# A two-layer decoder in fp32 on one core: up tiles of seven products stay in PSUM, and GpSimd makes one low half of the weights per up tile

## The chip, the cores and the metric

The kernel runs on one core of a Trainium2 chip. A core has five engines with a queue each: TensorE (PE, matrix products, which are written to PSUM alone), VectorE (DVE), ScalarE (ACT), GpSimd (POOL) and SyncE (SP, which here only starts DMAs). A queue runs its instructions in the order in which they stand. The metric is the device time of one execution in microseconds (us), as a median of several runs.

## The reference, cut to what matters

512 tokens of 1024 features pass two layers. Each has a token mixer, a gated MLP with a causal convolution, and a gated embedding. The change touches the MLP alone:

```python
def conv_ffn(xn, w_up, conv_w, conv_b, w_down):
    h = xn @ w_up                                    # 1024 -> 2 * 2816
    hp = jnp.pad(h, ((0, 0), (CONV_WIDTH - 1, 0), (0, 0)))
    c = conv_b + sum(hp[:, t:t + S] * conv_w[t] for t in range(CONV_WIDTH))   # width 3
    g, u = jnp.split(c, 2, axis=-1)
    return (jax.nn.silu(g) * u) @ w_down             # 2816 -> 1024
```

Everything is fp32.

## The kernel before

**Products in three matmuls.** Features lie on partitions and tokens along the free axis. Every operand x is kept as a high half (x rounded to a format that TensorE takes at full rate) and a low half (x minus that), and one product is three matmuls: high by high, high by low, low by high (`mm3`, line 234).

**Weights.** A table, `pieces`, lists every weight block in the order of its use. `load` brings a piece of up to 1 MB into one of three staging buffers (`wraw`, L173, queue SP). `pump` turns it into *units* of up to 128x1024, four units ahead of TensorE: ScalarE writes the high half (`wh`, L203), VectorE subtracts it for the low half (`wl`, L204). There are four buffers of each (WBUFS = 4), so a unit can be split only when TensorE has finished the one four before.

**Up tiles.** The MLP has 22 up tiles j per layer, each with 256 rows of `w_up`: 128 for the gate (s = 0) and 128 for the line (s = 1). Half of them (`UPS`: 7, 8, 9, 10, 12, 14, 16, 17, 18, 20, 21) are made by seven products of halves instead of eight, in `woven_up`; VectorE then also makes sums of weight blocks (`wsum`, L163 to L165). Products 1, 6, 7 and 4 are added up, in this order, in the left half of one PSUM bank (`ux`, in the code `chain`); 2 and 3, and 5, go to the halves of another (`uy`). After product 7 and after product 4 the running sum is read out by ScalarE with its sign turned (`minus`, L555), into an SBUF tile `line`; after products 1 and 6 it is copied into `head` (traced as `gate`). VectorE adds the rest (L816, L817). TensorE's order in such a tile is 1, 2, 6, 5, 7, 3, 4, twelve matmuls of 256 columns each. The other tiles have eight products' worth, 48 matmuls of 512 columns into the banks `up`, s = 0 first.

**Convolution.** `gated` takes the two halves, in PSUM for the ordinary tiles and in SBUF for those by seven products: ScalarE writes c = w2 * x + b (L761), VectorE adds two shifted taps to it (L763), for s = 0 and then for s = 1. Silu (L769), and VectorE's product with the line (L770), give the activation `a`.

**Down projection.** The tiles go in three parts: 0 to 7, 8 to 15 and 16 to 21. For the first two, activations are paired: `Pair.begin` and `Pair.end` make differences of the halves of two tiles (`act_3t`, `act_3u` for the fourth pair) and split each into high and low halves (ScalarE L311, VectorE L312). `woven_add` then takes seven products again, into `dx` and `dy`. Before it runs, the first up tile of the next part (8, and 16) is made with `later=True`: its products come before the down projection, its convolution inside it. The third part goes through `dense_add` (`d`), whose last factor is the activation of tile 21.

**What sets the order.** The code is recorded once, and a scheduler puts each engine's instructions in an order by its own estimate of times; `behind` adds an order between two instructions without a wait. At the seam of parts 1 and 2 it mixes the matmuls of tile 8 with the first ones of `dx` and `dy`. PSUM has eight banks, taken in turn.

Names in the profile leave out the numbers of buffers: `wl` is any unit's low half.

Of the kernel before, what the change touches and what calls it, by code (L numbers as in the profile page):

```python
# [13 lines left out]
P = 128  # L14
D = 1024
S = 512
# [7 lines left out]
ASIDE = {7: 12, 9: 7, 17: 7, 20: 6}  # L24
# [28 lines left out]
def tile_yoco(ctx: ExitStack, tc: tile.TileContext, t, out: bass.AP, out_b: bass.AP):  # L53
# [86 lines left out]
    raws, ready, splits, sums = {}, {}, {}, {}  # L140
    state = {"raw": 0, "unit": 0, "next": 0, "tags": [0, 1, 2], "turn": 2, "pt": 0, "sent": {}}
# [13 lines left out]
    def weave(i, q):  # L155
# [10 lines left out]
        return (g[:, 0:3:2], sums[i][:, 2:4], sums[i][:, 0:2], g[:, 3:4])[q]  # L166

# [11 lines left out]
    def pump(upto):  # L179
        while state["unit"] < min(upto, len(units)):  # L180
# [23 lines left out]
            state["split"] = splits[u] = cast, nc.vector.tensor_sub(low, src, hi.bitcast(F32))  # L204
# [77 lines left out]
    for i in range(IDLE):  # L282
        nc.tensor.matmul(ps, idle, idle.rearrange("p (o t) -> p o t", o=1).to_broadcast([P, 4, P]),
                         start=True, stop=True)
    minus_half = const.tile([P, S // 64], F32, name="minus_half")
# [445 lines left out]
    def ffn(l, norm, nxt):  # L731
# [23 lines left out]
        def gated(j, pss, fronts=()):  # L755
            cs = []
            for s, ps in enumerate(pss):
                col = s * NJ + j
                cw = [v("conv_w", (l * 3 + i) * 2 * NJ + col) for i in range(3)]
                c = tp.tile([P, S], F32, tag=f"c{s}", name=f"c{j}_{s}")  # L760
                nc.scalar.activation(c, ps, AF.Identity, bias=v("conv_b", l * 2 * NJ + col), scale=cw[2])  # L761
                for tap in (1, 2):
                    ins = nc.vector.scalar_tensor_tensor(c[:, tap:], ps[:, : S - tap], cw[2 - tap], c[:, tap:],  # L763
                                                         op0=ALU.mult, op1=ALU.add)
# [23 lines left out]
        def woven_up(j, later):  # L788
# [853 lines left out]
```

## Time and profile before

| | |
|---|---|
| median of 3 runs | 1098.21 us (1097.75 to 1098.51) |
| the profiled execution's own time | 1098.29 us |
| its span | 1096.6 us, granted TensorE clock 0.998 |
| busy: PE / DVE / ACT / POOL | 1087.3 / 958.1 / 660.1 / 124.9 us |
| low halves `wl` on DVE (two groups of the page) | 217.4 + 102.7 us in 198 + 84 instructions |
| first MLP, up tiles to the end of the down projection | about 156 to 498 us |
| second MLP | about 700 to 1045 us |

A row of the profile's tables reads: line, engine, operation, output <- inputs, shapes, count, busy time, mean duration of one in ns, idle time of the engine before them and what ended it. In a timeline, a row has its start, its duration, and in brackets the idle time before it. A matmul's row is longer than the distance to the next one, since matmuls overlap.

### The profile page before, as it was taken

To read this page: it belongs to the slowest core of one execution; us is meant where nothing else is said; L and a number is where in the kernel's file an instruction comes from. 1 tells how busy PE (TensorE), PEld (TensorE's weight loads), DVE (VectorE), ACT (ScalarE), POOL (GpSimd) and SP (SyncE) were. 2 spreads that over 40 slices of the span, in tenths; PEclk is the share of its full clock that TensorE was granted. 3 is DMA by queue.
4 is the path that set the end of the run, shared out by engine and by line. 5 is a ranking of instruction groups with operands and counts; after the bars stand their busy time and mean duration, and the time that the engine had idled before them with its cause. 6 is when DMAs were issued, how large, how long until landed. Compare 5 with 4: busy or idle time off the path is not lost.

```text
span 1096.6 us, 17486 instructions
## 1 busy us (share of the span) xinstructions
PE 1087.3 (99%) x6629; PEld 974.9 (89%) x6629; DVE 958.1 (87%) x1540; ACT 660.1 (60%) x1141; POOL 124.9 (11%) x192
## 2 busy tenths in 40 slices
PE   9999999999999999999999999999999999999997
PEld 7888988899999999988888887888999989999886
DVE  5598889989899989977988997799998999899787
ACT  5744665566576656655656775565665666567544
POOL 2200200000100010021114452000001000100200
PEclk9999999999999999999999999999999999999999
DMA  8621684124633267353234216441255333674634
GB/s 311 123 83 39 172 271 138 55 77 117 154 115 110 85 162 217 122 193 113 66 88 135 78 58 220 183 154 39 77 143 127 116 116 85 156 221 143 203 94 99
DMA packets 47508, 144.24 MB, mean 132 GB/s; under 512 B 13048, under 2 KB 18688, under 8 KB 36928
## 3 DMA queue, kind: packets, MB, share of 16 engines
q1 hardware_dynamic: 40560, 128.77, 35.7%
q0 software_dynamic: 5296, 9.70, 6.6%
q10 hardware_dynamic: 1568, 4.65, 1.1%
q8 instruction: 52, 0.85, 0.3%
q14 instruction: 32, 0.26, 0.1%
HBM read 116.89 MB, written 18.88 MB: 124 GB/s over the span
## 4 chain that ended last, share of the span: by engine, by line
PE 92%; DVE 2%; SPq 2%; issue 2%; DMA 1%; ACT 1%; POOL 0%; POOLq 0%; DVEq 0%; ACTq 0%
PE up L234 20%; PE ux L234 12%; PE dx L234 10%; PE uy L234 9%; PE dy L234 7%; PE d L234 4%; PE q L234 4%; PE gate L234 4%; PE u L234 4%; PE o L234 4%; PE up L751 2%; SPq L1399 2%; PE pv L1331 1%; PE v L244 1%; PE v L245 1%
## 5 line engine op out<-in xcount | busy, mean ns | idle before, releaser
L204 DVE TENSOR_TENSOR wl<-wraw,wh 128x1024 fp32r<-128x1024 f32 (+2 forms) x198 | 217.4, 1103 | 43.9 <-ACT wh L203 40.9
L203 ACT CAST wh<-wraw 128x1024 fp32r<-128x1024 f32 (+2 forms) x197 | 182.7, 932 | 105.8 <-PE up L234 21.5
L203 ACT CAST wh<-wsum 128x1024 fp32r<-128x1024 f32 x84 | 88.3, 1051 | 55.3 <-issue 14.9
L204 DVE TENSOR_TENSOR wl<-wsum,wh 128x1024 fp32r<-128x1024 f32 x84 | 102.7, 1226 | 17.7 <-ACT wh L203 14.3
L763 DVE SCALAR_TENSOR_TENSOR c<-up,vec,c 128x511 f32<-128x511 f32 (+1 forms) x88 | 65.1, 745 | 1.9 <-ACT c L761 1.5
L234 PE MATMUL up<-nf00h,wh 128*128 128x512 f32 x160 | 62.3, 390 | 0.0
L234 PE MATMUL up<-nf10h,wh 128*128 128x512 f32 x160 | 62.3, 390 | 0.0
L234 PE MATMUL up<-nf10l,wh 128*128 128x512 f32 x160 | 62.3, 389 | 0.0
L234 PE MATMUL up<-nf00l,wh 128*128 128x512 f32 x160 | 62.3, 389 | 0.0
L234 PE MATMUL up<-nf00h,wl 128*128 128x512 f32 x160 | 62.1, 389 | 0.0
L234 PE MATMUL up<-nf10h,wl 128*128 128x512 f32 x160 | 62.0, 389 | 0.0
L599 POOL DMA_DIRECT2D saved<-head x16 | 13.9, 870 | 412.5 <-DVE head L721 303.1
L163 DVE TENSOR_TENSOR wsum<-wraw 128x1024 f32<-128x1024 f32 x42 | 51.3, 1221 | 1.5 <-DMA wraw<-in_w_up 0.9
L761 ACT ACTIVATE c<-up,vec 128x512 f32<-128x512 f32 x44 | 33.9, 776 | 29.5 <-PE up L234 24.3
L234 PE MATMUL ux<-t,wh 128*128 128x256 f32 x264 | 50.8, 285 | 0.0
L234 PEld LDWEIGHTS ux<-t,wh 128*128 128x128 f32 x264 | 41.1, 192 | 0.8 <-ACT line L555 0.6
L234 PE MATMUL ux<-t,wl 128*128 128x256 f32 x132 | 37.4, 283 | 0.0
L234 PEld LDWEIGHTS up<-nf10h,wl 128*128 128x128 f32 x160 | 30.0, 188 | 6.3
L234 PEld LDWEIGHTS up<-nf00h,wl 128*128 128x128 f32 x160 | 30.0, 188 | 6.3
L234 PEld LDWEIGHTS up<-nf00l,wh 128*128 128x128 f32 x160 | 30.1, 188 | 6.1
L234 PEld LDWEIGHTS up<-nf10h,wh 128*128 128x128 f32 x160 | 30.0, 188 | 6.1
L234 PEld LDWEIGHTS up<-nf00h,wh 128*128 128x128 f32 x160 | 30.0, 188 | 6.1
(769 smaller groups left out, 3736.8 us busy)
## 6 DMA issues: line engine op xcount, KB each, us to landing
wraw<-in_w_up SPq DMA_DIRECT2D x44, 1024.0 KB, 5.1
wraw<-in_w_down SPq DMA_DIRECT2D x16, 1024.0 KB, 4.9
wraw<-in_w_gate SPq DMA_DIRECT2D x8, 1024.0 KB, 5.5
wraw<-in_w_down SPq DMA_DIRECT2D x8, 768.0 KB, 4.4
wraw<-in_w_u SPq DMA_DIRECT2D x4, 1024.0 KB, 9.2
wraw<-in_w_out SPq DMA_DIRECT2D x4, 1024.0 KB, 5.2
saved<-head POOLq DMA_DIRECT2D x16, 256.0 KB, 4.1
saved<-tail POOLq DMA_DIRECT2D x16, 256.0 KB, 4.1
```

The source lines that it names most:

```text
L163: nc.vector.tensor_add(s[:, 0::3], g[:, 1:2].to_broadcast([P, 2, k, P]), g[:, 0::3])
L203: cast = nc.scalar.copy(hi, src)
L204: state["split"] = splits[u] = cast, nc.vector.tensor_sub(low, src, hi.bitcast(F32))
L234: return [nc.tensor.matmul(ps, w, x, start=first and j == 0, stop=last and j == len(todo) - 1, skip_group_check=onto) for j, (w, x) in enu ...
L244: nc.tensor.matmul(ps, xh[:, s], wh[:, a:b], start=st, stop=False)
L245: nc.tensor.matmul(ps, xl[:, s], wh[:, a:b], start=False, stop=False)
L599: box["onto"] = nc.gpsimd.dma_start(x, y, accum_op=ALU.add)
L751: nc.tensor.matmul(ps, w[:, off + s * P : off + (s + 1) * P], x, start=k == 0 and x is xh and w is wh, stop=k == KD - 1 and x is xl)
L761: nc.scalar.activation(c, ps, AF.Identity, bias=v("conv_b", l * 2 * NJ + col), scale=cw[2])
L763: ins = nc.vector.scalar_tensor_tensor(c[:, tap:], ps[:, : S - tap], cw[2 - tap], c[:, tap:], op0=ALU.mult, op1=ALU.add)
L1331: nc.tensor.matmul(ps, lhs, rhs, start=j == 0, stop=j == len(todo) - 1)
L1399: nc.sync.dma_start(y[SQ * b : SQ * (b + 1), :, a, :], x[SQ * a : SQ * (a + 1), b::NQ].rearrange("p b m d -> p b (m d)"))
```

## The change

1. **Tiles by seven products stay in PSUM.** ScalarE's read-outs after product 7 is now a plain copy within the bank `ux`, from its left half to its right one. The one after product 4 is gone: the sum stays where it is. VectorE adds `side` and `head` in place, in PSUM (the first of them only after product 4 has ended). The line therefore keeps its sign, and `minus_w`, a negated copy of the convolution weights, made once by GpSimd, is used for it. The SBUF tiles for four of these outputs (`ASIDE`) are gone.
2. **One low half per up tile moves to GpSimd.** Except for tiles 6, 8, 15 and 16, the next unit's low half is a GpSimd subtraction that starts together with the taps (36 in all: 18 in each layer, of which 17 are 128x1024 and one 128x768). VectorE copies one column to `sign` when ScalarE has written the line's c, and GpSimd waits for that copy.
3. **The taps of these tiles stand together**, with high priority, in the order s = 0, s = 1, s = 0, s = 1, all behind `sign`, thus behind both of ScalarE's results.
4. Two small GpSimd instructions elsewhere (`prs`, `rows`) are put behind the last moved subtraction.

```diff
+OPEN = (6, 15)
@@ pump
-            state["split"] = splits[u] = cast, nc.vector.tensor_sub(low, src, hi.bitcast(F32))
+            held = low, src, hi.bitcast(F32)
+            if state["keep"] == u:
+                state["held"], state["keep"], splits[u] = held, None, (cast, None)
+            else:
+                start = shadows.pop(u, None)
+                lows = lowered(held, start) if start else nc.vector.tensor_sub(*held)
+                state["split"] = splits[u] = cast, lows
@@ new
+    def after(ins, front):
+        tc.add_manual_dep(ins.ins, front.ins.name,
+                          mybir.DependencyInfo(mybir.DependencyClass.Sync, mybir.DependencyReason.DATA),
+                          reason="start")
+    def lowered(held, start):
+        ins = box["lowered"] = nc.gpsimd.tensor_sub(*held)
+        after(ins, start)
+        return ins
@@ gated
+                if s and j in UPS:
+                    cw = [minus_w[:, (l * 3 + i) * NJ + j : (l * 3 + i) * NJ + j + 1] for i in range(3)]
                 nc.scalar.activation(c, ps, AF.Identity, bias=v("conv_b", l * 2 * NJ + col), scale=cw[2])
-                for tap in (1, 2):
-                    ins = nc.vector.scalar_tensor_tensor(c[:, tap:], ps[:, : S - tap], cw[2 - tap], c[:, tap:],
-                                                         op0=ALU.mult, op1=ALU.add)
-                    if fronts and tap == 1:
-                        behind(ins, splits[fronts[s]][1])
+                taps += [(c, ps, tap, cw[2 - tap]) for tap in (1, 2)]
...
+            if fronts or j in OPEN:
...
+            else:
+                with tc.high_priority():
+                    ins = nc.vector.tensor_copy(sign, cs[1][:, :1])
+                    if j in UPS:
+                        lowered(state["held"], ins)
+                    else:
+                        shadows[state["unit"]] = ins
+                    for x in taps[::2] + taps[1::2]:
+                        ins, front = tap(*x), ins
+                        behind(ins, front)
@@ woven_up
-            chain, other = psum(f"ux{j}")[:, first], psum(f"uy{j}")
-            if j in ASIDE:
-                head, tail = couple(ASIDE[j], f"out{j}", F32)
-            else:
-                head, tail = (tp.tile([P, S], F32, tag="hs", name=f"{x}{j}") for x in ("gate", "line"))
+            line, other = psum(f"ux{j}"), psum(f"uy{j}")
+            chain = line[:, first]
+            head = tp.tile([P, S], F32, tag="hs", name=f"head{j}")
...
             product(7, chain, w, 0, first=False)
-            minus(tail[:, second], chain)
+            nc.scalar.copy(line[:, second], chain)
             product(3, other[:, second], w, n, first=False)
-            product(4, chain, unit(), 0, first=False)
-            minus(tail[:, first], chain)
-            nc.vector.tensor_sub(tail[:, second], tail[:, second], side)
-            nc.vector.tensor_add(head, head, other)
-            return (head, tail) if later else gated(j, (head, tail))
+            if not later and j not in OPEN:
+                state["keep"] = state["unit"]
+            ends = product(4, chain, unit(), 0, first=False)
+            nc.vector.tensor_add(other, other, head)
+            after(nc.vector.tensor_add(line[:, second], line[:, second], side), ends[-1])
+            return (other, line) if later else gated(j, (other, line))
```

**What moves on VectorE.** This is VectorE's queue at the seam of parts 1 and 2 in the first layer, while TensorE makes tile 8: the rest of tile 7 (`c7`, `a7`), the pair's differences and low halves (`act0_3t`, `act0_3u`, `act0_3_0` to `_2`), the weight sums for `dx` (`wsum28`) and the low half of the first down unit (`wl59`). Before:

```order
L763 SCALAR_TENSOR_TENSOR c7_1_2429<-out7_2306,vec_84,c7_1_2429 128x511
L163 TENSOR_TENSOR wsum28_2487<-wraw28_2483 128x2x512
L763 SCALAR_TENSOR_TENSOR c7_1_2429<-out7_2306,vec_84,c7_1_2429 128x510
L164 TENSOR_TENSOR wsum28_2487<-wsum28_2487,wraw28_2483 128x512
L770 TENSOR_TENSOR a7_2433<-a7_2433,c7_1_2429 128x512
L165 TENSOR_TENSOR wsum28_2487<-wsum28_2487,wraw28_2483 128x512
L532 TENSOR_TENSOR act0_3t_2301<-a7_2433,a6_2297 128x256
L533 SCALAR_TENSOR_TENSOR act0_3u_2439<-act0_3t_2301,a7_2433 128x256
L204 TENSOR_TENSOR wl59_2486<-wraw28_2483,wh59_2485 128x1024
L535 SCALAR_TENSOR_TENSOR act0_3u_2439<-act0_3u_2439,a7_2433 128x256
L312 TENSOR_TENSOR act0_3_0_2436<-a7_2433,act0_3_0_2436 128x512
L312 TENSOR_TENSOR act0_3_1_2437<-act0_3t_2301,act0_3_1_2437 128x512
```

There the third `wsum` and `wl59` stand ahead of all three low halves of the pair; another row for the third low half, and then the next `wl`, follow. Now:

```order
L220 TENSOR_TENSOR wl58_2463<-wraw27_2350,wh58_2462 128x512
L805 TENSOR_TENSOR a7_2442<-a7_2442,c7_1_2434 128x512
L169 TENSOR_TENSOR wsum28_2495<-wraw28_2491 128x2x512
L550 TENSOR_TENSOR act0_3t_2310<-a7_2442,a6_2306 128x256
L551 SCALAR_TENSOR_TENSOR act0_3u_2448<-act0_3t_2310,a7_2442 128x256
L170 TENSOR_TENSOR wsum28_2495<-wsum28_2495,wraw28_2491 128x512
L553 SCALAR_TENSOR_TENSOR act0_3u_2448<-act0_3u_2448,a7_2442 128x256
L330 TENSOR_TENSOR act0_3_0_2445<-a7_2442,act0_3_0_2445 128x512
L330 TENSOR_TENSOR act0_3_1_2446<-act0_3t_2310,act0_3_1_2446 128x512
L171 TENSOR_TENSOR wsum28_2495<-wsum28_2495,wraw28_2491 128x512
L330 TENSOR_TENSOR act0_3_2_2447<-act0_3u_2448,act0_3_2_2447 128x512
L220 TENSOR_TENSOR wl59_2494<-wraw28_2491,wh59_2493 128x1024
```

Ahead of these stand the four taps of tile 7 in a row, and `wl57`, which stood before the first tap, is gone to GpSimd. `wl58` has come behind the taps, and `wl59` behind all three low halves of the pair and the third `wsum`.

**What moves on TensorE.** The matmuls of the same place, from the end of tile 8's product 3 (`uy8`), before:

```order
L234 MATMUL uy8_2450<-nf00l7_1001,wh57_2406 128x256
L234 MATMUL uy8_2450<-nf00h7_1000,wl57_2407 128x256
L234 MATMUL dx0_2567<-edge0_1756,wl59_2486 128x256
L234 MATMUL dx0_2567<-edge0_1756,wh59_2485 128x256 x2
L234 MATMUL dx0_2567<-edge0_1756,wl59_2486 128x256
L234 MATMUL dx0_2567<-edge0_1756,wh59_2485 128x256 x2
L234 MATMUL dx0_2567<-edge0_1756,wl59_2486 128x256
L234 MATMUL dx0_2567<-edge0_1756,wh59_2485 128x256 x2
L234 MATMUL dx0_2567<-edge0_1756,wl59_2486 128x256
L234 MATMUL dy0_2568<-act0_0_0h_1844,wl59_2486 128x256
L234 MATMUL ux8_2449<-t06_1957,wh58_2454 128x256
L234 MATMUL ux8_2449<-t07_1958,wh58_2454 128x256
```

Ten matmuls of `dx0` (of which the first reads `wl59`) and one of `dy0` stand between product 3 and product 4 (`ux8<-t...`). Now:

```order
L251 MATMUL ux8_2458<-t06_1963,wh58_2462 128x256
L251 MATMUL ux8_2458<-t07_1964,wh58_2462 128x256
L251 MATMUL ux8_2458<-t06_1963,wl58_2463 128x256
L251 MATMUL ux8_2458<-t02_2141,wh58_2462 128x256
L251 MATMUL ux8_2458<-t03_2142,wh58_2462 128x256
L251 MATMUL ux8_2458<-t02_2141,wl58_2463 128x256
L251 MATMUL ux8_2458<-t0_m5_1772,wh58_2462 128x256 x2
L251 MATMUL ux8_2458<-t0_m5_1772,wl58_2463 128x256
L251 MATMUL ux8_2458<-t0_rh_1949,wh58_2462 128x256
L251 MATMUL ux8_2458<-t0_rl_1950,wh58_2462 128x256
L251 MATMUL ux8_2458<-t0_rh_1949,wl58_2463 128x256
L251 MATMUL dx0_2574<-edge0_1760,wl59_2494 128x256
```

Product 4's twelve matmuls come first, one `dy0` matmul behind product 3, and the ten of `dx0`, beginning with `wl59`, behind them. Tile 8 of the second layer has the same two orders.

More of the change, by code (lines that the diff above doesn't have):

```diff
@@ L23 @@
 UPS = (7, 8, 9, 10, 12, 14, 16, 17, 18, 20, 21)
-ASIDE = {7: 12, 9: 7, 17: 7, 20: 6}
+OPEN = (6, 15)
 PAIRS = 4
@@ L139, in tile_yoco @@
     units = [(i, q, lo, n) for i, p in enumerate(pieces) for q, (lo, n) in enumerate(p[2])]
-    raws, ready, splits, sums = {}, {}, {}, {}
-    state = {"raw": 0, "unit": 0, "next": 0, "tags": [0, 1, 2], "turn": 2, "pt": 0, "sent": {}}
+    raws, ready, splits, sums, shadows = {}, {}, {}, {}, {}
+    state = {"raw": 0, "unit": 0, "next": 0, "tags": [0, 1, 2], "turn": 2, "pt": 0, "sent": {}, "keep": None, "held": None}
     def behind(ins, front):
@@ L284, in tile_yoco @@
                          start=True, stop=True)
+    sign = const.tile([P, 1], F32, name="sign")
     minus_half = const.tile([P, S // 64], F32, name="minus_half")
@@ L755, in gated @@
         def gated(j, pss, fronts=()):
-            cs = []
+            cs, taps = [], []
             for s, ps in enumerate(pss):
@@ L1427, in tile_yoco @@
     whole_f = whole.bitcast(F32)
-    nc.gpsimd.memset(rows.bitcast(F32), 0.0)
+    behind(nc.gpsimd.memset(rows.bitcast(F32), 0.0), box["lowered"])
     def bias_rows():
```

13 lines of the change are left out of this document (12 added, 1 removed).

## The prediction

> **What bounds the kernel now.** I read the page's busy totals first, then the waits of TensorE over the whole trace, then the two MLPs as windows.
>
> ```profile
> PE 1087.3 (99%) x6629; PEld 974.9 (89%) x6629; DVE 958.1 (87%) x1540; ACT 660.1 (60%) x1141; POOL 124.9 (11%) x192
> ...
> PE 92%; DVE 2%; SPq 2%; issue 2%; DMA 1%; ACT 1%; POOL 0%; POOLq 0%; DVEq 0%; ACTq 0%
> ```
>
> ```profile
> PE idle L283 <- DVE minus_half L286: 1.1, 1, 1.1
> PE dx L234 <- ACT head L701: 0.5, 1, 0.5
> PE sc L1263 <- PE sc L1264: 0.2, 1, 0.2
> ```
>
> ```profile
> 160.00:498.00 338.00, 338.00 (x2243) 312.17 (x2242) 307.68 (x426) 206.27 (x323) 21.00 (x23) 1.00 0.43 131
> 704.00:1045.00 341.00, 341.00 (x2256) 314.65 (x2256) 313.81 (x439) 209.27 (x329) 21.33 (x22) 1.00 0.44 132
> ```
>
> TensorE carries 92% of the chain of waits and itself waits 1.1 + 0.5 + 0.2 = 1.8 us in the whole run. In the windows (busy PE, PEld, DVE, ACT, POOL, then the clock) it is busy for all of 338.00 and 341.00 us at full clock. VectorE is at 307.68 of 338 us, 91%, but nobody waits for it there. Taking work from VectorE can therefore gain nothing; what the change can do is make TensorE wait. So I look for places where TensorE now gets its operand just in time and the new order delivers it later.
>
> **The change part by part.** *No more and no less for TensorE*: the same matmuls, hence 0.
>
> *VectorE's relief*: 34 low halves of 1024 and 2 of 768 columns, at the starting distance of such a subtraction (1.22 us for 1024; some 0.9 for 768), are 34 x 1.22 + 2 x 0.9 = about 43 us off VectorE. They lie beside matmuls: 0. ScalarE's 22 dropped read-outs: 0 for the same reason.
>
> *GpSimd's subtractions.* The trace has none of 1024 columns. The nearest rows:
>
> ```profile
> L1155 POOL TENSOR_TENSOR diff<-vd,diff 128x64 fp32r<-128x64 f32 x12 | 4.1, 355 | 0.2
> ```
>
> ```profile
> 522.50 1.33 POOL L342 TENSOR_TENSOR n1acc<-n1acc,n1sq 128x512 f32<-128x512 f32 x1 [3.85 <-ACT n1sq L337]
> 537.02 1.29 POOL L342 TENSOR_TENSOR n1acc<-n1acc,n1sq 128x512 f32<-128x512 f32 x1 [3.83 <-ACT n1sq L337]
> ```
>
> From 64 to 512 columns it is (1.29 - 0.355) / 448 = 2.1 ns a column, so 1024 columns take 1.29 + 512 x 0.0021 = 2.4 us. What runs beside them matters:
>
> ```profile
> 522.60 2.32 DVE L204 TENSOR_TENSOR wl<-wraw,wh 128x1024 fp32r<-128x1024 f32 x1
> ...
> 537.06 0.68 DVE L925 TENSOR_TENSOR z<-gate,np0rstd 128x512 f32<-128x512 f32 x1
> ```
>
> Both run beside a GpSimd addition. The subtraction with both sources in SBUF took 2.32 us, 1.1 more than its kind; the product that reads PSUM took its usual 0.68. The taps now read PSUM, and four of them take 4 x 0.66 = 2.64 us, longer than the 2.4. So I cost the pairing at 0. If GpSimd overhangs by up to 0.5 us, VectorE's next instruction is late by as much; at most tiles nobody notices: even where two tiles with seven products follow each other, the moved unit is wanted four products later (4 x 1.44 = 5.8 us after the end of product 4), and GpSimd ends at about 1.4 + 2.4 = 3.8. As bounds: 0, and 0.5 us at a place that is already late.
>
> *Taps from PSUM instead of SBUF.* These rows give both sources:
>
> ```profile
> L763 DVE SCALAR_TENSOR_TENSOR c<-up,vec,c 128x511 f32<-128x511 f32 x44 | 32.7, 746 | 1.6 <-ACT c L761 1.5
> L763 DVE SCALAR_TENSOR_TENSOR c<-gate,vec,c 128x511 f32<-128x511 f32 x14 | 10.5, 749 | 0.0
> ```
>
> 746 ns from PSUM (`up`) and 749 from SBUF (`gate`): no difference, 0. The Trainium skill, "VectorE: DVE Perf Modes", section "The TRN2 errata — SBUF-src ops pay a fixed extra latency per instruction", gives a vector instruction 58 cycles of access from SBUF and 120 from PSUM, by my estimate 65 ns more per tap at its 0.96 GHz, or 0.26 us per layer at the place below, and about 1101.6 us. The two rows show none of it.
>
> *Place A: the seam of parts 1 and 2, in each layer.* Here tile 7's convolution, the pair's differences and the first down unit meet. Before, in TensorE's chain, in TensorE's timeline, and on VectorE and ScalarE (first layer):
>
> ```profile
> 238.74 2.87 PE ux L234 x24
> ...
> 249.26 1.25 PE dx L234 x10
> ```
>
> ```profile
> 248.98 0.28 PE L234 MATMUL uy<-nf00h,wl 128*128 128x256 f32 x1
> 249.10 0.36 PE L234 MATMUL dx<-edge,wl 128*128 128x256 f32 x1
> ...
> 250.46 0.44 PE L234 MATMUL ux<-t,wh 128*128 128x256 f32 x2
> ```
>
> ```profile
> 240.93 0.75 DVE L763 SCALAR_TENSOR_TENSOR c<-out,vec,c 128x511 f32<-128x511 f32 x1
> 241.59 0.69 DVE L204 TENSOR_TENSOR wl<-wraw,wh 128x512 fp32r<-128x512 f32 x1
> ...
> 243.52 1.22 DVE L163 TENSOR_TENSOR wsum<-wraw 128x1024 f32<-128x1024 f32 x1
> 244.65 0.75 DVE L763 SCALAR_TENSOR_TENSOR c<-out,vec,c 128x510 f32<-128x510 f32 x1
> 245.31 0.69 DVE L164 TENSOR_TENSOR wsum<-wsum,wraw 128x512 f32<-128x512 f32 x1
> 245.92 0.69 DVE L770 TENSOR_TENSOR a<-a,c 128x512 f32<-128x512 f32 x1
> ...
> 247.12 0.42 DVE L532 TENSOR_TENSOR act_3t<-a,a 128x256 f32<-128x256 f32 x1
> 247.46 0.42 DVE L533 SCALAR_TENSOR_TENSOR act_3u<-act_3t,a 128x256 f32<-128x256 f32 x1
> 247.80 1.22 DVE L204 TENSOR_TENSOR wl<-wraw,wh 128x1024 fp32r<-128x1024 f32 x1
> ```
>
> ```profile
> 248.10 1.05 ACT L203 CAST wh<-wsum 128x1024 fp32r<-128x1024 f32 x1
> 249.44 0.62 ACT L311 CAST act<-act_3u 128x512 fp32r<-128x512 f32 x1 [0.28 <-DVE act_3u L535]
> 249.96 0.38 ACT L555 ACTIVATE line<-ux 128x256 f32<-128x256 f32 x1
> ```
>
> `wl59` ended at 247.80 + 1.22 = 249.02 and TensorE took it at 249.10: no slack. Product 4 of tile 8 must not overwrite what ScalarE reads out at 249.96 to 250.34; the ten `dx` matmuls ahead of it hid that, so it came at 250.46 without waiting.
>
> Now the same seconds with the new order. One matmul of 256 columns takes 0.12, twelve 1.44 (2.87 for 24). The result of tile 7's product 4 is out at 238.74 + 1.435 = 240.18, as before. On VectorE everything hangs on it, for the last addition waits for it, both results of ScalarE wait for that, and `sign` stands ahead of all four taps:
>
> - addition 0.42: to 240.64; ScalarE's c from PSUM, 0.776 (row below): to 241.46; `sign`, and the first tap at 241.59
> - four taps at a distance of 0.66 (240.93 to 241.59): to 244.23
> - `wl58` at 0.61 and `a` at 0.60 (245.31 to 245.92, 245.92 to 246.52): to 245.43
> - `wsum` at 1.13 (243.52 to 244.65): to 246.56
> - two differences at 0.34 (247.12 to 247.46): to 247.24
> - second `wsum` 0.60, `act_3u` 0.34, low halves 0 and 1, third `wsum`, low half 2, each 0.60: to 250.58
> - `wl59` 1.22: **ends at 251.80**
>
> ```profile
> L761 ACT ACTIVATE c<-up,vec 128x512 f32<-128x512 f32 x44 | 33.9, 776 | 29.5 <-PE up L234 24.3
> ```
>
> That is 2.8 us later than 249.02, since before, VectorE did `wsum`, `wl57` and `wl58` between the first taps and left the three low halves until after `wl59`. TensorE's new order asks for it later by product 4's 1.44, at 249.10 + 1.44 = 250.54. Without any other wait the loss is 251.85 - 250.54 = **1.31 us** (0.05 for the signal). Part of it comes earlier: product 4, now at 249.10, waits for ScalarE, whose queue has the cast of `wh60` (which needs the second `wsum`, 247.93 to 249.0), the cast of `act_3u` (to 249.54) and only then the copy within `ux` (to 249.82). So product 4 starts at 249.87, 0.77 late, ends at 251.31, and `dx` waits the remaining 0.54. The two overlap in the sum: 1.31, not 2.1. Two layers: 2 x 1.31 = **2.62 us**. Bounds: each of the seventeen steps may be 0.05 us shorter or longer, 0.45 to 2.2 per layer; the three low halves after the pair alone, 1.8, are what `wl59` lost its place to, so I keep 1.31. `wl57`, now on GpSimd from about 241.6 to 244.0, is wanted with product 7's third matmul, at 246.0 (product 3 ends at 249.10, ahead of it four single matmuls and twelve more: 249.10 - 1.44 - 0.48 - 1.44 = 245.74, and two more): 2 us of slack.
>
> *Place B: tile 21 ahead of `dense_add`, in each layer.* No pair, but TensorE's next part needs tile 21's activation.
>
> ```profile
> 465.43 32.67 PE d L234 x144
> ```
>
> ```profile
> 469.62 0.69 DVE L770 TENSOR_TENSOR a<-a,c 128x512 f32<-128x512 f32 x1
> ```
>
> ```profile
> 470.35 0.62 ACT L311 CAST act21h<-a 128x512 fp32r<-128x512 f32 x1 [2.48 <-DVE a L770]
> 470.88 0.83 ACT L203 CAST wh<-wraw 128x768 fp32r<-128x768 f32 x1
> ```
>
> `d` has 144 matmuls in 32.67, 0.227 each; 30 of them come ahead of the first that needs `act21h`: 465.27 + 6.81 = 472.08. Before, it was there at 470.97. Now the chain from 465.43 is: addition to 465.89, c to 466.71, taps from 466.84 to 469.48, `wl` of 768 columns (0.87) to 470.35, `a` to 471.05; ScalarE has the cast of 0.83 ahead of `act21h`, which TensorE lets go only at about 470.9, so `act21h` is ready at 472.0 to 472.26: between 0 and 0.2 late. I take 0.1 per layer, **0.2 us**; bounds 0, and 1.0 if that `wl`, with both sources in SBUF, runs beside GpSimd as in the row at 522.60.
>
> *Sum*: 2.62 + 0.2 = 2.8. The profiled execution took 1098.29 us, so 1101.1; the runs' median lies 0.08 below that execution: **1101.0 us**, 0.26% slower.
>
> **The rivals.** (1) *Not slower: VectorE catches up at place A.* If additions and taps from PSUM, and what follows them, are each 0.08 us shorter than my rows, seventeen steps make up 1.3 us, `wl59` is ready by 250.5, and `dx` never waits. Product 4's wait also has to shrink, or lie in time that `wl59` would cost anyway. It decides as soon as `wl59` ends by 250.5; time 1098.0 to 1098.7, no change; faster only by a share of the 1.8 us of waits. Against it: 746 against 749. (2) *GpSimd costs more than it takes.* If a subtraction takes 3 us or more, or VectorE gets slower beside it, tile 7's rest, place B and the tiles where two with seven products follow each other all shift; 0.5 us at A and 0.6 more at B in each layer: 2.2 on top, 1103.3. For it: 2.32 at 522.60; against it: 0.68 at 537.06, and taps that last longer than 2.4. The Trainium skill, "SBUF — State Buffer", section "Who interferes with whom", says of the port that VectorE and GpSimd share that whoever starts first holds it for its whole instruction, against a VectorE instruction with two sources in SBUF and not against one with a single one. Both rows above agree with that; by it a subtraction of 3 us would hold `wl58` until GpSimd's end, 0.4 us at place A, and the taps not at all. (3) *Half the loss:* VectorE's steps are 0.03 us shorter each, by which `wl59` comes 0.5 earlier and only the copy within `ux` is still felt, some 0.8 per layer: 1.6, 1099.9. (4) *PSUM runs short.* Outputs stay in their banks for about 14 us instead of being read out. With two banks of eight per tile they come round after four tiles, 4 x 10 us (seven products of 1.44), so I price it at 0; if it did bind at tile 8, whose banks wait longest, TensorE would wait for taps by 2 us or more per layer, 1102 and above.
>
> **How the numbers follow.** Forecast (both terms, within half a microsecond or so): 0.50. Rival 3: 0.22. Rival 2: 0.16. Rival 1: 0.09. Rival 4: 0.03. The likeliest gives 1101.0. Rival 1 and the low ends of place A would come below 1099.2, about 0.12 together; above 1103.8 lie the upper part of rival 2 and rival 4, 0.08. So 1099.2 to 1103.8 holds 8 in 10. A measurement of this kernel can tell 0.2%, 2.2 us, from no change: that is 1100.4. Slower by more than that: the forecast's 0.50 and rivals 2 and 4, 0.69; from the upper part of rival 3 another 0.05, 0.74. Faster by more than 2.2 us exceeds the 1.8 us that TensorE waits at all: 0.02. The rest, 0.24, is no change.
>
> **What would show it.** In the changed kernel's waits of TensorE, two new lines: `ux` behind ScalarE's copy within `ux`, 0.8 twice, and `dx` behind VectorE's `wl`, 0.5 twice, at 249 to 252 and at 795 to 798 us. In VectorE's timeline, `wl59` ends at 251.8. GpSimd shows 34 subtractions near 2.4 us, taps stay at 0.745 and VectorE's busy time falls to about 915 us. A first `d` matmul on `act21h` at 472.1 to 472.3 shows place B right. The forecast is wrong if TensorE does not wait around 250 and 796, or if new waits stand elsewhere: at the start of product 7 or of other tiles it would be GpSimd.

## The result

The changed kernel takes **1104.32 us** (median of 4 runs, 1103.71 to 1104.88), the kernel before 1097.98 us beside it: ratio 1.0057, 95% interval 1.004 to 1.0075. It is slower by 6.3 us. The forecast was slower by 2.8 us, 1101.0, with a range of 1099.2 to 1103.8: the sign is right, the size is under half, and the time lies outside the range.

The profiled execution took 1104.15 us (before: 1098.29). Its busy totals, and then all the waits of TensorE:

```profile
PE 1089.1 (99%) x6629; PEld 974.2 (88%) x6629; DVE 924.3 (84%) x1540; ACT 652.8 (59%) x1119; POOL 214.5 (19%) x229
```

```profile
PE d L251 <- ACT act21h L329: 1.5, 2, 0.8
PE ux L251 <- ACT ux L845: 1.4, 2, 0.7
PE idle L300 <- DVE minus_half L304: 1.1, 1, 1.1
PE dx L251 <- DVE wl L220: 0.6, 2, 0.3
```

VectorE was relieved by 34 us and nobody gained by it. Three of the four waits are new, each is there twice, once per layer: the two of the seam (`ux`, `dx`), which were forecast, and one on `act21h`, which was forecast at a tenth of its size. The rows understate them, since a row counts from where the modelled end of the last matmul lies. So I measure a pause from start to start of two matmuls, less the 0.12 us (256 columns) or 0.227 us (512) that they are apart otherwise. TensorE's timeline of the first layer, at the seam and then at the start of tile 21:

```profile
249.04 0.28 PE L251 MATMUL dy<-act_0l,wh 128*128 128x256 f32 x1
250.03 0.50 PE L251 MATMUL ux<-t,wh 128*128 128x256 f32 x2 [0.71 <-ACT ux L845]
250.37 0.28 PE L251 MATMUL ux<-t,wl 128*128 128x256 f32 x1
...
251.44 0.28 PE L251 MATMUL ux<-t_rh,wl 128*128 128x256 f32 x1
252.04 0.39 PE L251 MATMUL dx<-edge,wl 128*128 128x256 f32 x1 [0.32 <-DVE wl L220]
252.26 0.28 PE L251 MATMUL dx<-edge,wh 128*128 128x256 f32 x1
...
459.48 0.28 PE L251 MATMUL uy<-t,wh 128*128 128x256 f32 x1
459.88 0.50 PE L251 MATMUL ux<-t,wh 128*128 128x256 f32 x2
460.21 0.28 PE L251 MATMUL ux<-t,wl 128*128 128x256 f32 x1
```

From 249.04 to 250.03 are 0.99 us instead of 0.12: a pause of 0.87. From 251.44 to 252.04 are 0.60: 0.48. From 459.48 to 459.88 are 0.40: 0.28, a pause that the table of waits does not show at all. And behind each pause the first matmul is followed by the second one 0.10 us late: `ux` has two matmuls from 250.03 to 250.37, 0.34 instead of 0.24. This is a price of the pause too. Ahead of `act21h` the pause is 0.87 in the first and 0.99 in the second layer, again with 0.11 behind it.

| | first layer | second layer |
|---|---|---|
| A, seam behind tile 7: 0.87 + 0.48 + 2 x 0.10 | 1.55 | 1.55 |
| B, first matmul on `act21h` | 0.98 | 1.10 |
| C, product 6 of tile 21: 0.28 + 0.10 | 0.38 | 0.38 |
| first `up` to first `d` matmul, before and after | 311.49, 313.18 | 311.48, 313.18 |
| first `d` matmul to the end of the MLP, before and after | 32.67, 33.69 | 32.67, 33.81 |

The three places make 5.9 us. The two MLPs as wholes are 1.69 + 1.02 + 1.70 + 1.14 = 5.55 us longer (the kernel before had some 0.4 of small pauses there that are gone), out of 5.86 between the two profiled executions.

What made B is in the view of the other engines at tile 21 (VectorE, ScalarE, GpSimd, SyncE's DMA queue):

```profile
462.29 0.68 DVE L220 TENSOR_TENSOR wl<-wraw,wh 128x512 fp32r<-128x512 f32 x1
...
468.57 0.15 DVE L795 COPY sign<-c 128x1 f32<-128x1 f32 x1 [0.85 <-ACT c L781]
...
471.45 1.97 DVE L220 TENSOR_TENSOR wl<-wraw,wh 128x768 fp32r<-128x768 f32 x1
473.34 0.68 DVE L805 TENSOR_TENSOR a<-a,c 128x512 f32<-128x512 f32 x1
```

```profile
469.84 1.58 ACT L214 CAST wh<-wraw 128x768 fp32r<-128x768 f32 x2 [1.30 <-DMA wraw<-in_w_down]
...
474.05 0.62 ACT L329 CAST act21h<-a 128x512 fp32r<-128x512 f32 x1 [0.75 <-DVE a L805]
```

```profile
470.75 1.85 POOL L175 TENSOR_TENSOR wl<-wraw,wh 128x768 fp32r<-128x768 f32 x1 [8.44 <-DVE c L786]
```

```profile
463.14 0.33 SPq L496 DMA_DIRECT2D back<-saved  x1
463.63 0.33 SPq L184 DMA_DIRECT2D wraw<-in_w_down  x1
```

The transfer of this last one (its size, and the us from issue to landing):

```profile
wraw<-in_w_down SPq DMA_DIRECT2D x1, 768.0 KB, 6.1
```

`sign` lets GpSimd go at 468.7, but it starts only at 470.75: the cast that it needs waited until 469.84 for a load, started at 463.63. That load overwrites a staging buffer whose last reader, the `wl` of 512 columns at 462.29, now stands behind tile 20's four taps; one `back` stands ahead of it in the queue besides. So GpSimd no longer runs beside the taps from PSUM but beside the next `wl`, which has both sources in SBUF and takes 1.97 us instead of 0.95; `a`, and `act21h`, come by so much later. Counted from the first `d` matmul (467.01), this load starts at -3.38 us and lands at +2.74. Before the change the same load started at -7.77 and landed at -1.46.

### The profile page after: what moved, and what is told of

Its sections match the earlier page's. It is cut to its first block, busy times and chain, and to the rows that moved or that the text cites. A ratio compares the mean times of both kernels' runs of the same rounds, so it can differ in the third digit from the quotient of the medians.

```text
span 1102.4 us, 17525 instructions
## 1 busy us (share of the span) xinstructions
PE 1089.1 (99%) x6629; PEld 974.2 (88%) x6629; DVE 924.3 (84%) x1540; ACT 652.8 (59%) x1119; POOL 214.5 (19%) x229
## 4 chain that ended last, share of the span: by engine, by line
PE 89%; DVE 4%; DMA 2%; SPq 2%; issue 2%; ACT 1%; POOL 0%; POOLq 0%; DVEq 0%; ACTq 0%
PE up L251 20%; PE ux L251 11%; PE dx L251 10%; PE uy L251 8%; PE dy L251 7%; PE q L251 4%; PE gate L251 4%; PE u L251 4%; PE o L251 4%; PE d L251 4%; PE up L769 2%; SPq L1439 2%; PE pv L1371 1%; PE v L261 1%; PE v L262 1%
## 5 line engine op out<-in xcount | busy, mean ns | idle before, releaser
L220 DVE TENSOR_TENSOR wl<-wraw,wh 128x1024 fp32r<-128x1024 f32 (+2 forms) x176 | 193.6, 1103 | 37.4 <-ACT wh L214 36.8
L175 POOL TENSOR_TENSOR wl<-wraw,wh 128x1024 fp32r<-128x1024 f32 (+1 forms) x22 | 53.3, 2422 | 223.7 <-DVE sign L795 167.8
L220 DVE TENSOR_TENSOR wl<-wsum,wh 128x1024 fp32r<-128x1024 f32 x70 | 85.5, 1226 | 10.1 <-ACT wh L214 6.7
L786 DVE SCALAR_TENSOR_TENSOR c<-up,vec,c 128x511 f32<-128x511 f32 (+1 forms) x88 | 60.8, 742 | 0.5 <-ACT c L781 0.4
L175 POOL TENSOR_TENSOR wl<-wsum,wh 128x1024 fp32r<-128x1024 f32 x14 | 33.8, 2418 | 123.6 <-DVE sign L795 103.1
L804 ACT ACTIVATE a<-c 128x512 f32<-128x512 f32 x44 | 27.8, 632 | 29.1 <-DVE c L786 29.1
L795 DVE COPY sign<-c 128x1 f32<-128x1 f32 x36 | 5.6, 154 | 42.9 <-ACT c L781 42.9
```

Source lines behind the costliest of these rows:

```text
L175: ins = box["lowered"] = nc.gpsimd.tensor_sub(*held)
L220: lows = lowered(held, start) if start else nc.vector.tensor_sub(*held)
L786: return nc.vector.scalar_tensor_tensor(c[:, n:], ps[:, : S - n], w, c[:, n:], op0=ALU.mult, op1=ALU.add)
L804: box["silu"] = nc.scalar.activation(a, cs[0], AF.Silu)
```

## The experiments

All start from the changed kernel. In each comparison the kernel before stands beside it (1098.07 to 1098.22 us). The changed kernel was not run again with them, so gains are counted from its 1104.32, beside which the kernel before took 1097.98. The diffs are cut: lines that only note an instruction for later use are left out.

**1. Tile 7 alone goes back.**

```diff
-OPEN = (6, 15)
+OPEN = (6, 7, 15)
```

> Tile 7 alone goes back: its next low half stays on VectorE and its taps stand where the scheduler puts them; its outputs still stay in PSUM. Theory (the loss is made at three places per layer that do not depend on each other: 1.55 us at the seam behind tile 7, 0.38 us at the start of tile 21's product 6, 1.0 us ahead of the first matmul on act21h): the two waits of ux and dx near 250 and 796 us are gone or below 0.2 us, the other two places stay as they are, 1104.3 - 3.1 = 1101.2 us. Rival (GpSimd beside VectorE slows everything a little): under 1 us gained, 1103.3 us or more, with waits at the seam of over 0.5 us.

Measured 1102.65 us, ratio 1.0040 (1.0025 to 1.0055). Of the seam's pauses 0.13 + 0.10 is left, C stays at 0.38. But only 1.7 us were gained, since B grew to 1.62 and 1.90 us. That tile 7's new order makes A is confirmed, and B turned out to be nothing fixed; its load landed later here, at +3.50 and +3.77.

**2. The copy within `ux` first.** In tile 8 the cast of `wh60` is put behind ScalarE's copy.

```diff
-            nc.scalar.copy(line[:, second], chain)
+            turned = nc.scalar.copy(line[:, second], chain)
+            if j == 8:
+                behind(splits[state["next"] + 2][0], turned)
```

> In tile 8 alone ScalarE's copy within ux stands ahead of the cast of wh60. Theory (the low half wl59 sets the seam's end, the copy's wait lies inside its loss): the wait of ux near 250 us is gone, dx waits 1.3 to 1.5 us instead of 0.3 to 0.5, time unchanged, 1104.3 us within 0.5. Rival (the two waits add up, each with a cause of its own): dx still waits about 0.5 us, 0.9 us gained per layer, 1102.5 us.

Measured 1104.72 us, ratio 1.0059 (1.0044 to 1.0074): no gain. TensorE's timeline at the same place:

```profile
251.38 0.28 PE L251 MATMUL dy<-act_0l,wh 128*128 128x256 f32 x1
252.94 0.38 PE L251 MATMUL dx<-edge,wl 128*128 128x256 f32 x1 [1.29 <-DVE wl L220]
```

Product 4 runs without a pause, and `dx` pauses for 1.56 - 0.12 = 1.44 us in place of 0.87 + 0.48. So the seam's loss is set by when `wl59` is ready; the wait for the copy lay inside it, as the prediction had summed it.

**3. The order of the seam mended, tile 7 as in the change.** The copy first as in 2, and in tile 8 the three low halves of the pair behind `wl59` on VectorE.

```diff
+            for x in box.pop("lows", []) if j == 8 else []:
+                behind(x, splits[state["next"] + 1][1])
```

> In tile 8 alone ScalarE's copy within ux stands ahead of the cast of wh60, and the pair's three low halves stand behind wl59 on VectorE; GpSimd and tile 7's taps as in the change. Theory (the order behind tile 7's taps makes the seam's 1.55 us; wl59 then ends at 250.2 and is wanted at 250.6): no wait of ux or dx at the seam, 1104.3 - 3.1 = 1101.2 us; the wait on act21h stays by the landing rule, 0.7 to 1.9 us. Rival (GpSimd's subtraction behind tile 7 makes the seam late): dx still waits 0.5 us or more.

Measured 1102.37 us, ratio 1.0035 (1.0022 to 1.0048). Its waits:

```profile
PE d L251 <- ACT act21h L329: 2.4, 2, 1.2
PE idle L300 <- DVE minus_half L304: 1.1, 1, 1.1
PE dx L251 <- ACT head L723: 0.6, 1, 0.6
```

The `dx` row lies at 129 us, ahead of the first MLP, where the kernel before has it too. No wait at the seam is left in the table, with GpSimd and the taps in a row still there; pauses too small for it add up to 0.08 us in the first layer and 0.35 in the second. A is made by the order alone: three low halves that TensorE did not need yet, ahead of one that it was about to read. The time lies above the expected 1101.2 since B is 1.31 and 1.37 here.

**4. Read-out of product 1 first.** In tile 21 ScalarE's `head` stands ahead of the c of tile 20's line.

```diff
-            behind(box["silu"], nc.scalar.copy(head[:, first], chain))
+            behind(box["c" if j == 21 else "silu"], nc.scalar.copy(head[:, first], chain))
```

> ScalarE's read-out of tile 21's product 1 (head) stands ahead of the c of tile 20's line instead of behind it. Theory (product 6 waits for that read-out, which the two c's from PSUM have pushed back): the gap of 0.4 us near 459.5 and 1008.5 is gone, the waits at the seam and on act21h stay, 1104.3 - 0.8 = 1103.5 us. Rival (tile 20's convolution, 0.3 us later, pushes the rest back by as much): gap moved to the wait on act21h, 1104.3 us.

Measured 1103.03 us, ratio 1.0048 (1.0031 to 1.0065). ScalarE in the changed kernel, and here:

```profile
458.11 0.78 ACT L781 ACTIVATE c<-uy,vec 128x512 f32<-128x512 f32 x1
458.79 0.77 ACT L781 ACTIVATE c<-ux,vec,minus_w 128x512 f32<-128x512 f32 x1
459.46 0.37 ACT L833 COPY head<-ux 128x256 f32<-128x256 f32 x1
```

```profile
457.44 0.78 ACT L781 ACTIVATE c<-uy,vec 128x512 f32<-128x512 f32 x1
458.12 0.36 ACT L833 COPY head<-ux 128x256 f32<-128x256 f32 x1
458.38 0.79 ACT L781 ACTIVATE c<-ux,vec,minus_w 128x512 f32<-128x512 f32 x1
```

C is gone in both layers, A is unchanged, B is 0.73 and 0.96. So C is the read-out that stood behind two c's, which in turn wait for the additions in PSUM.

**5. Tile 20 alone goes back.** `OPEN = (6, 15, 20)`.

> Tile 20 alone goes back as tile 7 did above; tile 21 is left as in the change. Theory (GpSimd's subtraction at tile 20 holds a staging buffer about 3 us longer, so the load for the down projection starts late, its cast too, and GpSimd's next subtraction runs beside VectorE's wl of 768 columns): SP starts that load about 3 us earlier against the tiles, GpSimd's 768 columns start within 0.3 us of the first tap of tile 21, the wl of 768 behind the taps takes 0.95 us and not 1.97, the wait on act21h is 0.2 us or less: 1104.3 - 1.7 = 1102.6 us. Rival (the taps' chain alone makes act21h late): that wait stays 0.7 to 0.8, 1104.3 us.

Measured 1103.16 us, ratio 1.0046 (1.0032 to 1.0061). Half of it came as expected: the load starts 2.4 us earlier (-5.79), and the `wl` of 768 takes 0.95. But the pause on `act21h` did not go: 1.68 and 1.21 us. In this kernel's order ScalarE has the late cast ahead of both c's of tile 21, so that the whole convolution waits for the load (`sign` comes at +4.02 instead of +1.55). This run does not tell the collision from the taps; it shows the load as the cause of both. C is gone here too.

**6. The last reader of the load's buffer first.** One `wl` of 512 columns, the last that reads the staging buffer which the load overwrites, moves from behind tile 20's four taps to ahead of them.

```diff
+                        box.setdefault(("tap", l, j), ins)
@@ woven_up, behind its first unit()
+            if j == 21 and ("tap", l, j - 1) in box:
+                behind(box["tap", l, j - 1], splits[state["next"] + 2][1])
```

> One instruction moves in each layer: the low half of 512 columns for tile 21's last unit, the last reader of its staging buffer, stands ahead of tile 20's four taps on VectorE instead of behind them. Theory (the wait on act21h is set by the landing of the load that follows that reader; in the eight samples so far it is the landing, counted from the first d matmul, less 1.87 us): the load starts 2.6 us earlier and lands before +1.0 us, GpSimd's 768 columns start within 0.4 us of tile 21's first tap, the wl of 768 behind the taps takes 0.95 us instead of 1.97, the wait is below 0.15 us: 1104.3 - 2.0 = 1102.3 us. Rival (the taps in a row behind sign make act21h late by themselves): wait of 0.5 us or more, 1103.7 us or more.

Measured 1102.44 us, ratio 1.0039 (1.0024 to 1.0054). VectorE and GpSimd here:

```profile
459.20 0.68 DVE L220 TENSOR_TENSOR wl<-wraw,wh 128x512 fp32r<-128x512 f32 x1
459.80 0.74 DVE L786 SCALAR_TENSOR_TENSOR c<-uy,vec,c 128x511 f32<-128x511 f32 x1
...
471.05 0.95 DVE L220 TENSOR_TENSOR wl<-wraw,wh 128x768 fp32r<-128x768 f32 x1
```

```profile
468.64 1.86 POOL L175 TENSOR_TENSOR wl<-wraw,wh 128x768 fp32r<-128x768 f32 x1 [6.49 <-DVE sign L795]
```

The load behind that reader in SyncE's queue, its transfer, and the first of the two casts of what it brings:

```profile
459.95 0.33 SPq L184 DMA_DIRECT2D wraw<-in_w_down  x1
```

```profile
wraw<-in_w_down SPq DMA_DIRECT2D x1, 768.0 KB, 4.1
```

```profile
465.24 0.83 ACT L214 CAST wh<-wraw 128x768 fp32r<-128x768 f32 x1 [0.47 <-issue]
```

The load starts at -6.60, 3.2 us earlier (2.6 were expected), right behind the `wl` that was moved. It now goes ahead of the load that stood before it in the queue (that one starts at -4.37 and lands at +0.38, behind both casts) and is under way for 4.1 us instead of 6.1, so that it lands at -2.46. Both casts come ahead of tile 21's taps (465.24 and 466.81), GpSimd starts 0.22 us behind the first tap, as at the other tiles, `wl` takes 0.95, and B is 0 in both layers, with tile 21's taps in a row as in the change. So all of the expectation held. The twelve samples of B in which tile 21's order is that of the change give the rule, in us from the first `d` matmul:

| kernel | load lands, first and second layer | pause on `act21h` |
|---|---|---|
| the change | 2.74, 2.86 | 0.87, 0.99 |
| experiment 1 | 3.50, 3.77 | 1.62, 1.90 |
| experiment 2 | 3.18, 2.82 | 1.31, 0.97 |
| experiment 3 | 3.19, 3.24 | 1.31, 1.37 |
| experiment 4 | 2.60, 2.83 | 0.73, 0.96 |
| experiment 12 | 3.35, 2.99 | 1.48, 1.12 |
| experiment 6 (load started 3.2 us earlier) | -2.46, -2.44 | 0, 0 |

In the first twelve the pause is the landing less 1.87 us, within 0.02. The load starts at -3.38 or -3.39 in ten of them and at -3.22 or -3.23 in experiment 4, but is under way for 5.8 to 7.2 us, together with the loads of `back`. Why so different was not tried.

**7. All three mended.** 3, 4 and 6 together.

> The three mendings together (seam, head_first, early21), GpSimd and the taps in a row kept. Theory (the three places make all of the loss): no wait of TensorE in either MLP, 1098.0 us within 0.5, the same as before the change, not faster. Rival (a loss is left that no wait shows): 1099.3 us or more.

Measured 1099.49 us (10 runs, 1099.00 to 1101.61), ratio 1.0016 (1.0006 to 1.0025). A, B and C are gone from the profile, but it has one new wait, in tile 21:

```profile
PE ux L251 <- POOL wl L175: 0.4, 2, 0.2
```

```profile
458.81 2.73 POOL L175 TENSOR_TENSOR wl<-wsum,wh 128x1024 fp32r<-128x1024 f32 x1 [9.18 <-DVE sign L799]
```

GpSimd's subtraction now starts beside the `wl` that was put ahead of the taps, takes 2.73 instead of 2.42, and product 6 pauses for 0.36 + 0.10 us: 0.9 for the two layers. The two MLPs are 0.66 us longer than before, out of 0.72 between the two profiled executions; the rest of the 1.4 us between the medians is not assigned.

**8. Only the PSUM part.** No tile gives a low half to GpSimd.

```diff
-OPEN = (6, 15)
+OPEN = tuple(range(22))
-            behind(ins, box["lowered"])
+            "lowered" in box and behind(ins, box["lowered"])
-    behind(nc.gpsimd.memset(rows.bitcast(F32), 0.0), box["lowered"])
+    nc.gpsimd.memset(rows.bitcast(F32), 0.0)
```

> Only the first part of the change is left: outputs stay in PSUM with negated weights for the line, but no low half goes to GpSimd, and the taps stand where the scheduler puts them; the two small GpSimd instructions are not tied to anything. Theory (the loss comes from the taps in a row and what they push back): none of the three waits, 1098.0 to 1099.0 us. Rival (what stays in PSUM costs by itself, by banks held longer or taps slower from PSUM): 1100.5 us or more, with waits at product starts in many tiles.

Measured 1099.41 us (10 runs), ratio 1.0010 (1.0001 to 1.0019). The waits are those of the kernel before (1.1, 0.5, 0.2). From the first `up` to the first `d` matmul it has 311.85 and 311.84 us instead of 311.49 and 311.48: 0.36 per layer, in pauses of 0.06 to 0.16 us ahead of products of tiles 8, 10 and 12, with 0.10 more behind the two largest. So the PSUM part, in the order that the scheduler gives it, costs a little by itself: 0.7 of the 1.3 us between the medians is in such pauses, and the interval allows 0.1 to 2.1 us in all. The time is 0.4 above the upper end of what was expected. Which of them are banks not yet free was not tried.

**9. The taps in a row without GpSimd.** In tiles by seven products the low half is made by VectorE right behind the last tap; the two small GpSimd instructions are untied as in 8.

```diff
-                    if j in UPS:
-                        lowered(state["held"], ins)
-                    else:
-                        shadows[state["unit"]] = ins
                     for x in taps[::2] + taps[1::2]:
                         ins, front = tap(*x), ins
                         behind(ins, front)
+                    if j in UPS:
+                        behind(nc.vector.tensor_sub(*state["held"]), ins)
```

> The taps stay in a row behind sign, but no low half goes to GpSimd: in tiles by seven products VectorE makes it right behind the last tap, in the others in its old place. Theory (the order on VectorE makes the seam late, GpSimd only the rest of tile 21): dx waits 1.7 to 2.0 us at the seam, since wl57 now stands there too, the wl of 768 columns takes 0.95 us and the wait on act21h is below 0.3 us; 1104.3 + 0.7 - 2.0 = 1103.0 us. Rival (GpSimd makes both): both gone, 1099 us.

Measured 1107.62 us, ratio 1.0085 (1.0071 to 1.0099), 4.6 more than expected.

```profile
PE dx L251 <- DVE wl L220: 6.7, 4, 2.1
PE d L251 <- ACT act21h L329: 0.5, 1, 0.5
```

The seam pauses for 1.98 and 2.25 us, about as expected; `act21h` for 0.61 and 0.17. What was not expected: the other seam, behind tile 15, pauses as well, 1.56 us in each layer, since its sums and `wl` also stand behind the pair's low halves and VectorE gets there later. In the second layer the pause of 2.25 us has a further price. The window behind it (busy PE, PEld, DVE, ACT, POOL, then the granted clock, the DMA share and GB/s):

```profile
804.20:807.60 3.40, 3.40 (x19) 3.40 (x18) 3.40 (x5) 2.01 (x4) 0.00 (x0) 0.51 0.02 5
```

The clock is at 0.51 there, and sixteen distances of matmuls are 0.21 us instead of 0.12, some 1.5 us more; behind the 1.98 us of the first layer the clock stayed at 1.00. The other seam (3.3 us with its restarts) and this stretch are 4.8 together, close to the 4.6. So GpSimd does not make the loss at the seams; it takes away part of what the order costs there. Place B is another matter: without GpSimd `wl` takes 0.96, and VectorE waits 0.45 us for the cast of the late load ahead of it.

**10 and 11. Tiles 20 and 21 go back**, once with tile 7 (`OPEN = (6, 7, 15, 20, 21)`) and once with tile 7 kept and the seam mended as in 3 (`OPEN = (6, 15, 20, 21)`).

> Tiles 7, 20 and 21 go back (VectorE makes their low half, the scheduler places their taps); 30 of the 36 low halves stay on GpSimd and all outputs stay in PSUM. Theory (three places make the loss, the rest of the change costs nothing and gains nothing): no wait at any of the three places, 1098.0 to 1099.4 us, not faster than before the change. Rival (GpSimd costs at the other tiles too): 1100.5 us or more.

> Tiles 20 and 21 go back, tile 7 keeps GpSimd and its taps in a row, with the mended order at the seam (copy within ux ahead of the cast of wh60, the pair's low halves behind wl59). Theory: the same as with tile 7 gone back, 1098.0 to 1099.4 us, no wait at the seam, none on act21h, the gap at the start of tile 21's product 6 gone. Rival (GpSimd beside the seam costs): 0.7 us or more above it.

Measured 1100.07 us, ratio 1.0017 (1.0008 to 1.0026), and 1099.22 us, ratio 1.0010 (1.0001 to 1.0019). C is gone in both; at the seam 0.13 + 0.10 us per layer are left in experiment 10, as in experiment 1, and some 0.09 in experiment 11. B stays at 0.71 and 0.82, and 0.84 and 0.81: as in experiment 5 ScalarE has the cast that waits for the load ahead of tile 21's two c's.

```profile
465.16 0.83 ACT L214 CAST wh<-wraw 128x768 fp32r<-128x768 f32 x1 [1.00 <-DMA wraw<-in_w_down]
465.90 0.78 ACT L781 ACTIVATE c<-uy,vec 128x512 f32<-128x512 f32 x1
466.57 0.82 ACT L214 CAST wh<-wraw 128x768 fp32r<-128x768 f32 x1
467.36 0.78 ACT L781 ACTIVATE c<-ux,vec,minus_w 128x512 f32<-128x512 f32 x1
```

These are from the first of the two. That tile 7 costs nothing with GpSimd once the order is right is confirmed; that B would go with tiles 20 and 21 was wrong. None of the kernels here is faster than the one before.

**12. Taps from SBUF beside GpSimd.** In tiles 9 and 12 the sum of `head` and the other products goes to SBUF, so that taps one and three have both sources there.

```diff
-            nc.vector.tensor_add(other, other, head)
+            res = head if j in (9, 12) else other
+            nc.vector.tensor_add(res, other, head)
```

> In tiles 9 and 12 VectorE's sum of head and the other products goes to SBUF again, so the first and third tap have both sources in SBUF while GpSimd subtracts; the second and fourth still read PSUM. Theory (two sources in SBUF exclude GpSimd's instruction and the other way round, as at 522.60 us before the change): in these four tiles GpSimd starts about 0.5 us later, behind the first tap, and the third tap takes 1.8 to 2.6 us instead of 0.74, until GpSimd is done; the PSUM taps stay at 0.74. Rival (taps do not mind GpSimd): all four 0.74 us.

One run, 1106.75 us. VectorE and GpSimd at the first of the four tiles:

```profile
303.32 0.74 DVE L786 SCALAR_TENSOR_TENSOR c<-head,vec,c 128x511 f32<-128x511 f32 x1
303.98 0.75 DVE L786 SCALAR_TENSOR_TENSOR c<-ux,minus_w,c 128x511 f32<-128x511 f32 x1
304.64 2.24 DVE L786 SCALAR_TENSOR_TENSOR c<-head,vec,c 128x510 f32<-128x510 f32 x1
306.81 0.73 DVE L786 SCALAR_TENSOR_TENSOR c<-ux,minus_w,c 128x510 f32<-128x510 f32 x1
```

```profile
303.58 2.75 POOL L175 TENSOR_TENSOR wl<-wsum,wh 128x1024 fp32r<-128x1024 f32 x1 [9.87 <-DVE sign L795]
```

The third tap takes 2.24 us and ends at 306.88, after GpSimd's end at 306.33. The second, from PSUM, takes its 0.75 in the middle of GpSimd's instruction. GpSimd's row is 0.35 longer than elsewhere (2.75 against 2.40 to 2.44), not later, with the first tap ahead of it. All four tiles read the same (2.22 to 2.24). Most of the 2.4 us above the change are two more pauses of TensorE per layer, 0.61 and 0.48 us, in tile 10. So leaving the outputs in PSUM is what lets the taps run beside GpSimd at all. The Trainium skill, "SBUF — State Buffer", section "Who interferes with whom", says the same of instructions with one and with two sources in SBUF. The trace agrees: 0.75 us beside GpSimd with one, 2.24 with two.

## Why the prediction was right or wrong

**What bounds the kernel: right.** TensorE at 99%, and 34 us off VectorE gained nothing. The relief itself was put at 43 us, with VectorE at 915, and came to 33.8, at 924.3: `wl` takes 41.0 less, but 36 copies to `sign`, left out of that sum, take 5.5, and two weight sums beside GpSimd 4.2 (next paragraph). It made no difference.

**GpSimd's subtraction: right.** 2.4 us was forecast; 32 of the 34 of 1024 columns took 2.40 to 2.44. The other two (at 441 and 990 us) took 3.10: their cast came late, so that they ran beside VectorE's weight sums, and one such sum of 512 columns took 2.77 instead of 0.69. TensorE did not wait there. The group of 14 that read `wsum`, and the taps:

```profile
L175 POOL TENSOR_TENSOR wl<-wsum,wh 128x1024 fp32r<-128x1024 f32 x14 | 33.8, 2418 | 123.6 <-DVE sign L795 103.1 <-PE ux L251 20.5
L786 DVE SCALAR_TENSOR_TENSOR c<-uy,vec,c 128x511 f32<-128x511 f32 x22 | 16.3, 742 | 0.0
```

**Taps from PSUM: right.** 742 ns, most of them beside GpSimd, against 746 and 749 before. The 65 ns that the prediction estimated from the Trainium skill, "VectorE: DVE Perf Modes", section "The TRN2 errata — SBUF-src ops pay a fixed extra latency per instruction", are not there.

**Place A: right in its mechanism, 0.24 us short per layer.** `wl59` was to end at 251.80 and ended at 251.99 (the 0.19 are there at the first tap already, 241.78 instead of 241.59; all later steps fit), TensorE's two waits were to be 0.77 and 0.54 and were 0.87 and 0.48. The difference is 0.04 of pause and the 0.20 that the two restarts cost, of which the prediction knew nothing. That the waits overlap (experiment 2), and that the three low halves ahead of `wl59` are what it lost its place to (experiment 3), held.

**Place B: the step that failed.** "I take 0.1 per layer": it was 0.98 and 1.10, the end that had been written down as the bound, 1.0. The chain of VectorE from tile 21's product 4 was right (first tap at +1.63 us from the first `d` matmul, forecast +1.57, and experiment 6 shows that this chain makes no pause). What was wrong is the silent assumption in it that GpSimd starts with the taps, because the cast that it reads is there: it started 2.1 us later, beside `wl`, which took 1.97 us where the sum has 0.87. The prediction moved a `wl` of 512 columns behind four taps in its own sum for tile 7 and did not ask the same of tile 20: which load waits for its last reader, and what is queued on that DMA queue by then. This load started 4.4 us later against the tiles (-3.38 instead of -7.77) and landed 4.2 us later; it was under way about as long as before (6.1 and 6.3 us). Of the 3.1 us that the sum is short (5.9 instead of 2.8), B makes 1.9, C 0.8 and A 0.5.

**Place C: missing.** 0.38 per layer. The prediction counted ScalarE's queue at the seam and at `act21h`, but not at tile 21's start, where the c's of tile 20, now tied to additions in PSUM, stand ahead of a read-out that product 6 waits for. The place was not in the table of waits before, since there the read-out ended at 457.42 and product 6 began at 458.09 without a pause, with 0.7 us to spare.

**The rivals.** "GpSimd costs more than it takes" had a chance of 0.16 at 1103.3. What it said of place B, that VectorE gets slower beside GpSimd, happened, but not for its reason: no subtraction takes 3 us by itself; the one there takes 1.85 and came at the wrong time. That 1103.3 is nearer to the measured time than the forecast is partly luck: it adds 0.5 us per layer at A, where 0.24 came, and has no C. Nothing of "PSUM runs short" is seen at tile 8; the 0.36 us per layer of experiment 8 are the nearest to it.

## What to carry to other kernels

Where TensorE is never idle, moving work off another engine is worth only what its order does to the few operands that arrive just in time, so list those first. When instructions are tied together, follow the one that they push back to the end: the last reader of a staging buffer sets when a load starts, the load sets a cast, and the cast sets when the freed engine collides with the old one. Three mendings of the order got back 4.8 of the 6.3 us here; undoing the move for tiles 7, 20 and 21 got back 4.3, since the scheduler then made another order with a wait of its own.

## What the runs showed of the hardware

Behind every pause of 0.13 us or more in the MLPs of these runs TensorE's second matmul comes 0.10 us late: 0.22 instead of 0.12 us behind the first at 256 columns, 0.335 instead of 0.227 at 512. Behind one pause of 2.25 us the granted clock was 0.51 for 3.4 us (experiment 9), behind one of 1.98 us it was not lowered. VectorE and GpSimd excluded each other in these runs only where VectorE reads two sources in SBUF: a tap of 0.74 became 2.24, a `wl` of 0.95 became 1.97, and the taps with a source in PSUM stayed at 0.74. A load of 768 KB was under way for 4.2 us alone (in the change, -15.99 to -11.80 us from the first `d` matmul) and for 5.8 to 7.2 among the load ahead and those of `back`; by this spread alone place B cost 1.7 us in experiment 4 and 3.5 in experiment 1.
